# Another list order for one decoder step on one core: accumulator chains kept together, and eight small rows issued by ScalarE

## The chip, the cores and the metric

The kernel runs on one core of a Trainium2 chip. The metric is the device time of one execution in microseconds (us), as the median over runs. A core has five engines with instruction queues of their own: TensorE (PE in the profile; PEld is its weight load), VectorE (DVE), ScalarE (ACT), GpSimd (POOL) and SyncE (SP), which only issues transfers. SP, ACT and POOL can issue DMA transfers; the program chooses which.

## What is computed

One layer of a hybrid decoder, for a prompt of 512 tokens and for 8 sample rows of one token each, with model width 1024, all in f32:

```python
gate, q, k, v, z_att, logf, u, z_ssm = _pre(x, c, ...)   # adaLN RMSNorm, one projection, its columns split
o_att = fox_attention(q, k, v, logf)                     # 8 heads of 64, score bias from cumulated log-gates
y_ssm, h = s5_scan(u, h0, ...)                           # 32 groups, 64 complex states each
att = o_att * silu(z_att)
g   = gelu(y_ssm);  ssm = g * sigmoid(g @ w_glu + b_glu) * silu(z_ssm)
x   = x + gate * (concat(att, ssm) @ w_out)
y   = rmsnorm(x, g_final)
```

In prompt attention the score of query t and key s is `q·k/8 + cum[t] − cum[s]`, where `cum` is the running sum of the log-gates. Each sample row attends to 4096 cached positions, found through a page table, and to itself. The outputs are y, k, v, log-gates and the last states, for the prompt and for the sample.

## The kernel before, in words

**An order by list scheduling.** The body, `tile_fox_s5_step`, is written as plain generators: `prompt()` (norm, projections of q, k, v, u and the gates, S5, attention, output projection) and `decode()` (the sample rows). Their instructions are not issued at once. `Engine` records each call in a `Plan`, with the regions it reads and writes, a modelled duration and the ring buffers it uses. `Plan.order()` then picks the order: a simulation with a ready heap for each engine, where an engine that comes free takes the ready operation with the smallest key. The key is the operation's place in the written program, less `BEHIND` times the work that depends on it, plus `TURN[i // GRP]`, one number for each group of 20 operations. For PE there is one exception: if the smallest key asks for another tile shape (rows by columns of the array, each 32, 64 or 128) than the last product, PE takes a product of the present shape instead, provided its key is at most `STAY` greater. `LAT` holds for each engine two latencies: to a successor on another engine, and on the same one. A transfer is put off if 8 of its queue are under way. `Plan.issue()` emits everything in that order on line 381 (385 in the changed kernel), so every instruction of the profile carries this line, and groups are told apart by their tiles. The order within an engine is fixed in the program; engines meet only through semaphores, and an engine executes in order.

**The parts named later.** PSUM tiles are `mm` (two buffers, projections and outputs), `tr` (two, transposes), `s2` (one, scores, shown as `s`), `sm` and `pv` (one each). `hT` is the normalised transposed prompt, `w` and `qk` are weight buffers (the latter also hold q and k), `cs` the transposed conditioning vectors. `arA` and `arB` are two large SBUF areas, of which pieces are lent out by turns.

**Decode.** For each of 64 chunks of 1 MB (8 rows × 8), POOL gathers K rows by an indirect transfer (`kidx` holds the row numbers). DVE multiplies the chunk by the broadcast q (`kv<-kv,qs`, 128x2048) and reduces it to scores (`sc<-kv`). After the softmax, POOL gathers V chunks, and PE accumulates them in `pv`, four products of 128 rows by 32 columns each, in four column quarters. The broadcast q is itself a product, `sm<-qsp,s4b`, copied to `qs` by ACT. Gathers of the cached log-gates (`suf<-in_cache_logf_dram,lidx`) and their suffix sums give the score bias. Chunks lie in three `kva` buffers, and later also in pieces of arA.

**Prompt attention** (`attn`, from line 1174). DVE makes `cum` by a scan (line 1185) over transposed log-gates. For each pair of heads, m = 0 to 3, ACT copies q and k of two heads into two 66-row tiles in arB (line 1197), and a transfer (line 1198) puts two rows of `cum`, 4 KB, into row 64 of the q tile and row 65 of the k tile (eight transfers in all, `arB<-arA 1x2x512`, issued from SP). The products for the scores (`s2<-arB`) read these 66 rows. ACT takes exponentials, PE transposes them, and PE multiplies by v into an `mm` tile.

**The start.** The adaLN modulation is a product of `cs` with four slabs of `w_ada`, on `w_88` and `w_89` among them, in four column quarters. POOL raises the mean squares to the power −1/2 (`arA<-arA,nhalf`), ACT scales x by that, and PE transposes it (`tr<-ident,kv`).

Of the kernel before, what the change touches and what calls it, by code (L numbers as in the profile page):

```python
# [37 lines left out]
BEHIND = 0.0005  # L38
STAY = 150
GRP = 20  # L40
XAT = 5
TURN = [
# [6 lines left out]
]  # L49
# [22 lines left out]

LAT = {"PE": (200, 5), "DVE": (190, 127), "ACT": (165, 200), "Pool": (90, 100), "SP": (90, 0)}
ACT_SET = {AF.Exp: 0, AF.Silu: 1, AF.Sin: 1, AF.Gelu_apprx_tanh: 2, AF.Sigmoid: 3, AF.Identity: 1}
# [50 lines left out]
class Plan:  # L125
# [108 lines left out]
    def order(self):  # L234
# [24 lines left out]
        ready = {e: [] for e in engines}  # L259
        queue = deque(), deque()  # L260
        cols, loaded, hw = {}, 0.0, 0.0
# [24 lines left out]
        while done_n < n:  # L286
# [31 lines left out]
            if op.dma:  # L318

                q = queue[e == "Pool"]  # L320
                while q and q[0] <= t:
                    q.popleft()
                if len(q) >= 8:
                    heapq.heappush(waiting[e], (q[0], i))
                    continue
# [25 lines left out]
            if op.lock:  # L351
                t = max(t, port)
                port = t + c
            start[i] = t
            if op.func is not None and op.func != func:
# [4 lines left out]
            if op.dma:  # L360
                dma_free = max(dma_free, fin + 650) + op.dma
                fin = dma_free + 980
                queue[e == "Pool"].append(dma_free + 930)
            end = max(end, fin)
# [24 lines left out]
def tile_fox_s5_step(ctx, tc, x_prompt, x_sample, c_prompt, c_sample, cache_k, cache_v, cache_logf,  # L389
# [140 lines left out]
    t = trt()  # L530
# [643 lines left out]
    def attn(rp, ap):  # L1174
# [17 lines left out]
        for m in range(4):  # L1192
            qa, ka = qk
            for j in range(2):
                x = qk[j]
                for hh in range(2):
                    acopy(x[0:64, hh], res["qk"][j][64 * hh:64 * hh + 64, m])
                SP.dma_start(x[64 + j:65 + j], cum[2 * m:2 * m + 2])
            t = trt()
# [460 lines left out]
```

## Time and profile before

| what | value |
| --- | --- |
| time before, median of 3 runs | 613.65 us (605.77 to 616.77) |
| the profiled execution's own time | 612.74 us |
| span of its trace, first to last instruction | 610.7 us |
| mean granted PE clock | 0.933 |
| busy: PE, DVE, POOL, ACT | 529.8, 485.6, 227.6, 159.5 us |
| moved by DMA | 176.41 MB, mean 289 GB/s |

In the profile an instruction group reads "engine, operation, out<-in by the program's tile names without buffer numbers, shape, count". A bracket behind a timeline row is the engine's idle time just before it, and what ended it. The chain is followed back from the last instruction: each step goes to what released it. A 128x512 f32 product leaves two records. PE's granted clock is 1.00 at full speed.

### The profile page before, as it was taken

The numbers are of one execution on the slowest core, as the hardware profiler recorded it, in microseconds if no ns is written. First come the engines' busy times: TensorE is split into PE (matmuls) and PEld (weight loads), VectorE is DVE, ScalarE is ACT, GpSimd is POOL, SyncE is SP. The second block draws the span as 40 slices with busy tenths as digits, with TensorE's granted clock in tenths as the row PEclk, the third lists the DMA queues.
The fourth block names the chain that finished last, engine by engine and source line by source line (L and its number), as shares of the span: only waits on it lengthen the run. The fifth ranks groups of instructions, "written<-read, shape, count | busy, mean of one in ns | idle before, by whom it ended". The sixth has DMA issues, their size and how long they took to land.

```text
span 610.7 us, 7345 instructions
## 1 busy us (share of the span) xinstructions
PE 529.8 (87%) x2858; PEld 233.7 (38%) x2858; DVE 485.6 (80%) x687; ACT 159.5 (26%) x294; POOL 227.6 (37%) x172
## 2 busy tenths in 40 slices
PE   5538899999999798978887799889989989999993
PEld 2104477533333234646323344334334333333231
DVE  7985987997999999889562999886979376998514
ACT  4224303211001110150212563551542653000101
POOL 6670101452354133234411366324534251553400
PEclk9955989999999798999987899989968999999997
DMA  7996303583897659689695689988999999689940
GB/s 225 398 378 228 140 2 138 174 298 149 284 355 290 242 188 411 240 304 420 257 419 187 255 319 386 385 321 312 357 411 381 348 367 406 261 320 388 384 188 36
DMA packets 45195, 176.41 MB, mean 289 GB/s; under 512 B 6933, under 2 KB 21497, under 8 KB 27753
## 3 DMA queue, kind: packets, MB, share of 16 engines
q0 software_dynamic: 19264, 135.74, 57.6%
q1 hardware_dynamic: 25392, 39.44, 18.3%
q10 hardware_dynamic: 504, 0.78, 0.4%
q8 instruction: 22, 0.36, 0.2%
q14 instruction: 13, 0.10, 0.0%
HBM read 171.48 MB, written 4.42 MB: 288 GB/s over the span
## 4 chain that ended last, share of the span: by engine, by line
PE 41%; DVE 26%; DMA 16%; ACT 6%; issue 5%; POOL 3%; SPq 2%; DVEq 0%; POOLq 0%; ACTq 0%
PE mm L381 27%; DVE arA L381 9%; DVE sc L381 8%; PE pv L381 6%; DVE kv L381 5%; DMA kv<-in_cache_v_dram,kidx 5%; PE tr L381 4%; DMA arB<-arA 3%; DMA kv<-in_x_prompt_dram 3%; DMA out_dram<-e 2%; POOL arA L381 2%; ACT L381 2%; DMA arA<-in_cache_v_dram,kidx 2%; SPq L381 2%; PE s L381 2%
## 5 line engine op out<-in xcount | busy, mean ns | idle before, releaser
L381 PE MATMUL mm<-hT,w 128*128 128x512 f32 x256 | 134.6, 630 | 0.1
L381 DVE TENSOR_TENSOR kv<-kv,qs 128x2048 f32<-128x2048 f32 x38 | 86.4, 2280 | 15.0 <-DMA kv<-in_cache_k_dram,kidx 12.4
L381 POOL DMA_INDIRECT kv<-in_cache_v_dram,kidx x38 | 56.0, 1474 | 94.4 <-PE pv L381 36.3
L381 DVE TENSOR_REDUCE sc<-kv 128x32 f32<-128x2048 f32 x38 | 86.0, 2273 | 0.2
L381 POOL DMA_INDIRECT kv<-in_cache_k_dram,kidx x38 | 48.0, 1262 | 82.6 <-PE pv L381 36.7
L381 POOL DMA_INDIRECT arA<-in_cache_v_dram,kidx x26 | 50.5, 1941 | 67.2 <-DVE sc L381 55.5
L381 POOL DMA_INDIRECT arA<-in_cache_k_dram,kidx x26 | 39.0, 1498 | 95.5 <-PE pv L381 52.7
L381 DVE TENSOR_TENSOR arA<-arA,qs 128x2048 f32<-128x2048 f32 x26 | 59.2, 2279 | 2.9 <-DMA arA<-in_cache_k_dram,kidx 1.8
L381 DVE TENSOR_REDUCE sc<-arA 128x32 f32<-128x2048 f32 x26 | 59.1, 2275 | 0.2
L381 PEld LDWEIGHTS mm<-hT,w 128*128 128x128 f32 x256 | 41.9, 195 | 27.5 <-issue 22.8
L381 ACT ACT_TABLE_LOAD x31 | 39.8, 1283 | 36.5 <-DMA q_s<-in_x_sample_dram 11.1
L381 PE MATMUL pv<-kv,arA 128*32 128x512 f32 x304 | 42.1, 613 | 5.8 <-DMA kv<-in_cache_v_dram,kidx 5.8
L381 PE MATMUL s<-arB 128*32 128x128 f32 (+4 forms) x240 | 35.2, 306 | 7.0 <-DMA arB<-arA 5.6
L381 DVE TENSOR_TENSOR arA<-arA 128x512 f32<-128x512 f32 (+8 forms) x105 | 37.2, 378 | 0.6
L381 PE MATMUL mm<-w,hT 128*128 128x256 f32 x128 | 37.3, 410 | 0.0
L381 PE MATMUL pv<-arA 128*32 128x512 f32 x208 | 31.1, 655 | 6.6 <-DMA arA<-in_cache_v_dram,kidx 3.6
L381 ACT ACTIVATE arB<-tr 128x512 f32<-128x512 f32 (+3 forms) x44 | 20.3, 477 | 54.8 <-PE s L381 27.5
L381 PE MATMUL mm<-w,arB 128*128 128x512 f32 x64 | 33.2, 610 | 0.0
L381 PEld LDWEIGHTS s<-arB 128*32 128x32 f32 (+1 forms) x240 | 23.3, 152 | 24.5 <-issue 14.1
L381 PE MATMUL mm<-qk,arB 128*128 128x512 f32 x64 | 32.3, 607 | 0.0
L381 PE MATMUL mm<-qk,hT 128*64 128x256 f32 x256 | 32.1, 404 | 0.0
L381 PE MATMUL tr<-ident,arB 128*128 128x128 f32 (+1 forms) x102 | 24.4, 302 | 8.5 <-ACT arB L381 8.5
(244 smaller groups left out, 717.5 us busy)
## 6 DMA issues: line engine op xcount, KB each, us to landing
w<-in_w_in_dram SPq DMA_DIRECT2D x10, 1024.0 KB
w<-in_w_ada_dram SPq DMA_DIRECT2D x9, 1024.0 KB
qk<-in_w_ada_dram SPq DMA_DIRECT2D x2, 1024.0 KB
kv<-in_x_prompt_dram SPq DMA_DIRECT2D x2, 1024.0 KB
qk<-in_w_in_dram SPq DMA_DIRECT2D x2, 1024.0 KB
qk<-in_w_out_dram SPq DMA_DIRECT2D x2, 1024.0 KB
w<-in_w_out_dram SPq DMA_DIRECT2D x2, 1024.0 KB
hT<-in_x_prompt_dram SPq DMA_DIRECT2D x1, 2048.0 KB
```

The costliest lines, as they stand in the source:

```text
L381: fn(*args, **kw)
```

## The change

Five edits, none of which adds, removes or alters an operation, its operands or its arithmetic:

- `STAY` is 80 in place of 150, and all 113 numbers of `TURN` are others, on the whole larger in size.
- PE's latency to its own successor is 0 in place of 5. In the heap of `order()`, the next product of a chain is then ready at the moment PE chooses, and its key is close to that of the product before.
- The model of the DMA queues has one queue for each engine, where SP and ACT shared one.
- A transfer that POOL issues is modelled as held while DVE has the port that both use.
- The rows of `cum` are issued from ACT (`A`) and not from SP.

```diff
-STAY = 150
+STAY = 80
 GRP = 20
 XAT = 5
 TURN = [
-    -872, -5579, -1925, -3047, -2630, -3562, -2038, -2939, -2200, -1386, -1903, -48, -3522, -654, -1143, -30,
+    -7694, 3784, 245, 1458, -775, -289, 127, -5585, 3014, -1233, -3, -966, 1188, -487, -8884, 491, 5234, 987,
...
-LAT = {"PE": (200, 5), "DVE": (190, 127), "ACT": (165, 200), "Pool": (90, 100), "SP": (90, 0)}
+LAT = {"PE": (200, 0), "DVE": (190, 127), "ACT": (165, 200), "Pool": (90, 100), "SP": (90, 0)}
...
-        queue = deque(), deque()
+        queue = {e: deque() for e in engines}
...
-                q = queue[e == "Pool"]
+                q = queue[e]
...
             if op.lock:
                 t = max(t, port)
                 port = t + c
+            elif op.dma and e == "Pool":
+
+                c += max(0.0, port - t)
...
-                queue[e == "Pool"].append(dma_free + 930)
+                queue[e].append(dma_free + 930)
...
-                SP.dma_start(x[64 + j:65 + j], cum[2 * m:2 * m + 2])
+                A.dma_start(x[64 + j:65 + j], cum[2 * m:2 * m + 2])
```

What it does to the built programs is seen in the order of instructions on each engine. Three places follow; a number behind a name is the tile's number, and xN stands for N like instructions in a row.

PE, in the third head pair of prompt attention, before. `mm_413` is a gate projection, `s2_415` scores, `tr_408` and `tr_409` transposes (all of 128 by 128 tiles), `pv_359` V chunks (128 by 32):

```order
L381 MATMUL mm_413<-hT_110,w_380 128x512
L381 MATMUL pv_359<-kv_358,arA_78 32x512 x4
L381 MATMUL tr_408<-ident_91,arB_79 128x128
L381 MATMUL mm_413<-hT_110,w_380 128x512
L381 MATMUL pv_359<-arA_78 32x512 x4
L381 MATMUL tr_409<-ident_91,arB_79 128x128
L381 MATMUL mm_413<-hT_110,w_380 128x512
L381 MATMUL s2_415<-arB_79 128x128
L381 MATMUL mm_413<-hT_110,w_380 128x512
L381 LDWEIGHTS identb_95
L381 MATMUL s2_415<-maskb_96,identb_95 128x128
```

And the same place now:

```order
L385 MATMUL mm_413<-hT_110,w_380 128x512
L385 MATMUL tr_408<-ident_91,arB_79 128x128
L385 MATMUL mm_413<-hT_110,w_380 128x512
L385 MATMUL tr_409<-ident_91,arB_79 128x128
L385 MATMUL mm_413<-hT_110,w_380 128x512 x6
L385 MATMUL s2_415<-arB_79 128x128
L385 LDWEIGHTS identb_95
L385 MATMUL s2_415<-maskb_96,identb_95 128x128
L385 MATMUL s2_415<-arB_79 128x128 x2
```

The chain of `mm_413` and that of `s2_415` no longer alternate, and the two groups of V products between them have gone to a later place, where two such groups stand together.

PE, at the broadcast of the first sample row's q (`sm_150<-qsp_124,s4b_123`), before. `mm_166` to `mm_169` are the projection of u:

```order
L381 MATMUL mm_168<-qk_117,hT_110 64x256
L381 MATMUL mm_168<-qk_118,hT_110 64x256
L381 LDWEIGHTS s4b_123
L381 MATMUL sm_150<-qsp_124,s4b_123 128x512
L381 MATMUL mm_168<-qk_117,hT_110 64x256
```

And now:

```order
L385 MATMUL mm_166<-qk_117,hT_110 64x256
L385 MATMUL mm_166<-qk_118,hT_110 64x256
L385 MATMUL mm_156<-e2_155,s4_98 8x512
L385 LDWEIGHTS s4b_123
L385 MATMUL sm_150<-qsp_124,s4b_123 128x512
L385 MATMUL mm_166<-qk_117,hT_110 64x256
```

The broadcast stands behind the first two products of `mm_166`, where before it stood behind all of `mm_166` and `mm_167` and most of `mm_168`; in rows of PE it has gone from the 201st to the 76th.

SP, around the first two rows of `cum`, before:

```order
L381 DMA w_300<-in_w_in_dram 128x8x256
L381 DMA out_3_dram<-arA_78 128x4x512
L381 DMA w_301<-in_w_in_dram 128x8x256
L381 DMA arB_79<-arA_78 1x2x512 x2
L381 DMA out_8_dram<-arA_78 8x512
```

And ACT now, where they stand between activations of the S5 part:

```order
L385 ACTIVATE e2_276<-mm_275 128x256
L385 ACTIVATE arA_78<-mm_277 8x256
L385 ACT_TABLE_LOAD
L385 ACTIVATE arB_79<-mm_279,gcol_103 128x512
L385 DMA arB_79<-arA_78 1x2x512 x2
L385 ACTIVATE arB_79<-mm_282,gcol_103 128x512
L385 ACTIVATE arB_79<-mm_286,gcol_103 128x512
```

The other six rows of `cum` stand on ACT each behind the copies of q or k into the same tile (`arB_79<-qk`).

POOL does both of its powers ahead of the gathers `suf`, where all eight gathers came before the second power, and DVE computes `kidx` and `lidx` behind the first modulation of the sample rows, where it did so among its first instructions. At the start of PE's stream both `mm_111<-w_88,cs_102` and `mm_111<-w_89,cs_102` stand behind transposes of x (`tr_127<-ident_91,kv_85`), where `w_88` stood ahead of them.

11 rows, old and new, of the table TURN are left out of this document.

## The prediction

> **What bounds the kernel now.** I read the shares of the page first, then busy time by stage, then the chain of waits, and last the timelines of the places the change touches.
>
> ```profile
> PE 529.8 (87%) x2858; PEld 233.7 (38%) x2858; DVE 485.6 (80%) x687; ACT 159.5 (26%) x294; POOL 227.6 (37%) x172
> PE 41%; DVE 26%; DMA 16%; ACT 6%; issue 5%; POOL 3%; SPq 2%; DVEq 0%; POOLq 0%; ACTq 0%
> ```
>
> TensorE (PE) is busy for 87% of the span and carries most of the chain that ended last; VectorE (DVE) comes next with 80%, and transfers hold 16% of the chain. An average hides which of them rules where, so here are five stages (columns: us of the stage, then busy us and instructions of PE, weight loads, DVE, ACT and POOL, the granted PE clock, the share of the DMA engines and GB/s):
>
> ```profile
> 0.00:75.00 75.00, 46.31 (x370) 21.25 (x370) 61.94 (x198) 24.69 (x39) 33.53 (x37) 0.80 0.80 279
> 75.00:300.00 225.00, 207.83 (x1297) 104.73 (x1298) 204.59 (x287) 39.18 (x68) 79.63 (x50) 0.97 0.66 245
> 300.00:330.00 30.00, 21.87 (x69) 7.99 (x67) 12.04 (x9) 3.72 (x6) 3.75 (x4) 0.84 0.81 321
> 330.00:596.00 266.00, 249.28 (x1106) 98.61 (x1101) 201.04 (x185) 89.45 (x176) 109.18 (x77) 0.96 0.88 339
> 596.00:610.70 14.70, 4.47 (x25) 1.11 (x24) 6.01 (x11) 2.47 (x5) 1.48 (x4) 0.75 0.10 38
> ```
>
> Up to 75 us DVE leads (61.9 of 75). From 75 to 300 PE and DVE are both nearly full: PE idles 225 − 207.8 = 17.2 us, DVE 20.4. From 300 to 330 nothing is full, which is a stall. From 330 to 596 PE alone is full (249.3 of 266, 16.7 us idle), with DVE at 201. So time can come out of the PE's stream after 330 us, out of the stall, and, between 75 and 300 us, only to the extent that PE and DVE both have less to do or less to wait for.
>
> **No work is taken away.** Both programs have the same products, DVE instructions and table loads; the change only orders them otherwise and sends eight small rows through another queue. Four things follow.
>
> **1. Fewer changes of tile shape on PE.** Counted in the built orders, the accumulator changes from one product to the next 960 times before and 392 times now; the tile shape (rows by columns of the array: 128 by 128, 128 by 32 for the V products, and so on) changes 452 times before and 240 now. These two must be priced apart, and one piece of the PE's timeline does it:
>
> ```profile
> 553.33 1.02 PE L381 MATMUL mm<-qk,arB 128*128 128x512 f32 x2
> 554.19 1.02 PE L381 MATMUL mm<-w,arB 128*128 128x512 f32 x2
> 555.14 1.07 PE L381 MATMUL pv<-kv,arA 128*32 128x512 f32 x8
> 556.14 1.12 PE L381 MATMUL mm<-w,arB 128*128 128x512 f32 x2
> 557.10 1.02 PE L381 MATMUL mm<-qk,arB 128*128 128x512 f32 x2
> 557.96 1.02 PE L381 MATMUL mm<-w,arB 128*128 128x512 f32 x2
> 559.68 1.02 PE L381 MATMUL mm<-w,arB 128*128 128x512 f32 x2
> ```
>
> The rows with qk and with w go into two different accumulators, with the same tile shape. From 553.33 to 554.19 is 0.86 us, and from 557.10 to 557.96 again 0.86: alternating accumulators costs nothing (the f32 product leaves two records each time). So the change's most visible effect, chains that stay together, is worth 0.00 where the shape stays. A visit to the V products in between costs something: 554.19 to 555.14 is 0.95 instead of 0.86, so 0.09 for one change; and from 554.19 to 557.96 is 3.77 us for three products (3 × 0.86) and one V group (some 0.87, since four column quarters run side by side), 0.32 more than 3.45, so 0.16 for each of the two. I take 0.12 for a change, with 0.10 and 0.16 as ends.
>
> Where the changes go matters more than their number. 136 of the 212 stand before the stall and 71 behind it. Behind it PE is full: 71 × 0.12 = 8.5 us, of which I count 8, since part of the 16.7 us of idling there (waits on ACT and gathers) stays where it is; ends 71 × 0.10 = 7.1 and 71 × 0.16 = 11.4. Before it, 136 × 0.12 = 16 us of PE leaves a stretch in which DVE is as full as PE, so it comes out in point 3.
>
> **2. The stall at 318 to 330 us.** Prompt attention starts with products that need the rows of cumulated log-gates in partitions 64 and 65 of arB. Timeline and chain, in order of time:
>
> ```profile
> 296.01 0.39 SPq L381 DMA_DIRECT2D w<-in_w_in_dram  x1
> 296.52 1.21 DVE L381 TENSOR_TENSOR_SCAN arA<-ones,tr 8x512 f32<-8x512 f32 x1 [1.34 <-PE tr L381]
> 297.75 8.95 SPq L381 DMA_DIRECT2D arB<-arA  x2
> 304.11 19.71 DMA arB<-arA
> 308.40 2.29 DVE L381 TENSOR_TENSOR kv<-kv,qs 128x2048 f32<-128x2048 f32 x1 [5.55 <-DMA kv<-in_cache_k_dram,kidx]
> 323.95 0.77 PE L381 MATMUL s<-arB 66*128 66x128 f32 x2 [5.56 <-DMA arB<-arA]
> ```
>
> The scan that makes the rows ends at 297.7. SP, which has just issued a weight load of 1 MB, needs 8.95 us to issue two rows of 4 KB, and the rows land about 323.9, 26 us behind the scan. PE idles 5.56 us for them. It then pays again:
>
> ```profile
> 316.70:323.60 6.90, 1.70 (x10) 0.30 (x2) 4.54 (x3) 0.60 (x1) 0.00 (x0) 1.00 0.91 357
> 323.60:330.40 6.80, 6.45 (x18) 2.71 (x19) 1.29 (x4) 0.69 (x1) 0.00 (x0) 0.50 0.14 17
> 330.40:337.20 6.80, 6.80 (x30) 3.43 (x26) 2.08 (x6) 3.87 (x10) 1.88 (x2) 1.00 0.98 354
> ```
>
> After the window with 1.70 us of work the clock is 0.50 for 6.8 us, so that what was done there would have taken half: 3.4 us. The stall costs 5.56 + 3.4 = 9 us.
>
> The change issues the rows from ACT. What does ACT's queue need? Nothing of this kind goes through it before, and there are two sets of rows to bound it, the other six cum rows on SP and a pair of small loads on ACT:
>
> ```profile
> L381 SPq DMA_DIRECT2D arB<-arA x8: 564/958/6301, 297.8 to 443.9; - x8
> 258.77 0.80 ACTq L381 DMA_DIRECT2D arB<-in_b_ada_dram  x2
> 262.31 0.63 ACT L381 ACTIVATE arB<-qk 64x512 f32<-64x512 f32 x1 [4.55 <-DMA arB<-in_b_ada_dram]
> ACT L381 <- DMA q_s<-in_x_sample_dram: 11.1, 1, 11.1
> ```
>
> Issues take 0.56 to 6.3 us on SP, with a median of 0.96; a pair on ACT took 0.80, and its data were used 3.5 us after the issue (258.77 to 262.31). The other small ACT load was waited for 11.1 us. So the rows should be there 1 + 3.5 to 1 + 11 us behind the scan: 4.5 to 12. In the new order some 14 us of PE's stream (by the same prices) lies between the transposes that feed the scan and the first product that needs the rows; before it was about 20, since PE ran dry at 318.4. The cover is thinner, the rows quicker: the wait goes, and with it the cold clock. What is late next is DVE, which waited 5.55 us for a K chunk at 308.40 and had 12 us of work in 30. I take 8 of the 9 us, with 0 and 9 as ends.
>
> A page bears on this from the other side. The Trainium skill, "Trainium Kernel Development and Optimization", section "Key Constraints", says that transfers issued from SP, ACT and POOL all run on the same 16 DMA engines, and that issuing from several only saves issue time. The window with a DMA share of 0.91 fits it, and by it only the 9 us of issue would go; whether the rest of the lateness stays is a rival below.
>
> ACT is in order, and takes on eight issues. The first pair stands between two activations of the S5 part, the others each behind the copy that writes the same tile, which already waits for that tile's last reader; so they add no wait for a buffer, only their issue, six or so of 0.6 to 1 us on an engine with 89 of 266 us busy. No charge.
>
> **3. The decode begins earlier.** The first multiply of a K chunk needs the broadcast q, a product out of qsp:
>
> ```profile
> 75.87 0.42 DVE L381 CAST qsp<-e 8x512 bf16<-8x512 f32 x1
> 77.42 14.49 PE L381 MATMUL mm<-qk,hT 128*64 128x256 f32 x116
> 98.61 0.39 PE L381 MATMUL sm<-qsp,s4b 72*128 72x512 bf16 x1
> 99.67 2.29 DVE L381 TENSOR_TENSOR kv<-kv,qs 128x2048 f32<-128x2048 f32 x1 [0.47 <-ACT qs L381]
> ```
>
> qsp is there at 76.3, and PE makes the product at 98.6, behind a long projection. Now it stands ahead of that projection, so that the first K chunk can be multiplied from about 80, some 20 us earlier, and DVE work that stood ahead is put behind. DVE has 20.4 us of idling in 75 to 300, and PE 17.2 plus 16 from point 1; since the two must both shrink, the gain is 0 at least (the idle places move) and 16 at most. DVE's sum stays 204.6 and K chunks still wait for gathers, so I am near the lower end: 6.
>
> **4. The start.** One step goes the other way. The modulation needs the sums over both halves of w_ada before the first normalised rows are made.
>
> ```profile
> 33.67 10.22 POOL L381 TENSOR_SCALAR arA<-arA 128x4 f32<-128x4 f32 x1 [6.49 <-ACT hT L381]
> 37.08 1.94 PE L381 MATMUL mm<-w,cs 128*32 128x512 f32 x8 [1.09 <-DMA w<-in_w_ada_dram]
> 43.97 1.04 POOL L381 TENSOR_TENSOR arA<-arA,nhalf 128x4 f32<-128x4 f32 x1
> 48.73 1.93 PE L381 MATMUL mm<-w,cs 128*32 128x512 f32 x8
> 52.54 0.37 DVE L381 TENSOR_TENSOR arA<-tr,arA 128x72 f32<-128x72 f32 x2 [8.72 <-PE tr L381]
> ```
>
> One such group of four products ran at 37.08 while PE had nothing else, the other at 48.73 on the path, behind transposes of x that wait for POOL's reciprocal root (10.22 us for 128 by 4 values, up to when DVE's row of two-input operations ends). In the new order both groups stand behind the first transposes: 1.93 us more on the path. At best the group finds a gap again: 0. At worst POOL's second step is held as the first was and the group waits behind a further copy, 1.04 + 1.04 us: 4. I take 2. The gathers move as well. POOL had done its suffix gathers, 1.26 us apart, early on:
>
> ```profile
> 21.03 0.95 POOL L381 DMA_INDIRECT suf<-in_cache_logf_dram,lidx  x1 [0.30 <-issue]
> 22.29 0.96 POOL L381 DMA_INDIRECT suf<-in_cache_logf_dram,lidx  x1 [0.30 <-issue]
> ```
>
> Now they follow the second root and the index arithmetic, which DVE does behind the first modulation, by its place in the order an estimated 62 to 70 us. Six of them, 1.26 us apart, the K gather and its landing come before the first multiply: another reason for "about 80", and for no more than 6 in point 3.
>
> **Sum.** 2 − 6 − 8 − 8 = −20 us, from a span of 610.7 to 590.7. The profiled execution took 612.74, 2.04 around its span, so 592.7; it lies 0.9 under the median of the runs (613.65), so the figure stands for a median too: 593. The ends give 0 − 16 − 9 − 11.4 = −36.4 (576) and 4 − 0 − 0 − 7.1 = −3.1 (610).
>
> **Rivals.** *The savings are swallowed.* DVE stays as full as it was before 300 us, and waits for gathers as it did at 308.40 (5.55 us); point 3 is worth nothing, of the stall only the cold clock goes (3.4), and behind it 8 less the start's 2: −9.4, so 603, or 606 if the cold clock stays as well. For it: DVE at 204.6 of 225 and DMA shares of 0.66 to 0.88. Against: behind 330 us PE is the only full engine. Chance 0.17.
>
> *The rows land no sooner.* If they wait for what is already under way on the DMA engines and not for SP, they land 26 us behind the scan as before, and PE has work for 14: a wait of 12 in place of 5.56. That is 6.4 lost and 8 not gained: 607. For it: the DMA share of 0.91 just ahead. Against: the three later pairs on SP, for none of which PE waited, and ACT's 3.5 us. [...] Chance 0.10.
>
> *The decode starves at first.* If index arithmetic and gathers on POOL are held by DVE as the root was for 10 us, the first K multiply comes about 10 us after 99.67 and not 20 before it: 6 not gained and 10 lost, 609. For: the 10.22 us above. Against: by then DVE has other work to fill that time. Chance 0.10.
>
> *ACT is stopped by its new transfers: slower.* If a pair takes 8.95 us to issue on ACT as it did on SP, the exponentials behind it wait, and PE needs those for its next transposes. Four pairs: 4 × 8.95 = 35.8, so 628. It decides from about 2 us a pair on, since ACT's slack covers less than that during a head pair. For: the 6.3 us of one row. Against: the median of 0.96 and 0.80 for the pair on ACT. Chance 0.08.
>
> That leaves 0.55 for the forecast, with its own range of 576 to 610.
>
> **Chances.** 2% is about what a measurement of this kernel can tell from no change: under 601.4 is faster, over 625.9 slower. The forecast falls under 601.4 in 0.50 of its 0.55, the rest is within 2%; the swallowed savings and the next two rivals, which end at 603 to 609, put 0.08 under, 0.24 within and 0.05 over, by what the rest of a table of new places may add; the last is slower, 0.08. Together 0.58, 0.29 and 0.13. For 8 in 10 the range goes from 576 to 616.
>
> **What would show it.** Point 1: V visits between products in fewer, longer groups, and PE busy over less than 249 us behind the first prompt scores, with the same count. Were alternating accumulators dear after all, PE would lose more than 12 us there. Point 2: no idle time of PE on arB's DMA, no window at 0.50 in mid kernel, and ACT issues under 1 us. Point 3: the first K multiply near 80. Point 4: the two adaLN groups both behind the copies of x, and DVE's idle gap longer than 8.72. I am wrong if PE's idle time between 75 and 596 grows, whoever it is that it waits for, or if the first K multiply is later than 99.67 and the end moves with it.

## The result, and the profile after

| | before | after |
| --- | --- | --- |
| median | 611.16 us (605.77 to 616.77, 4 runs) | 572.97 us (569.87 to 580.62, 4 runs) |
| ratio of the two, 95% interval | | 0.9386 (0.9267 to 0.9504) |
| profiled execution, its span | 612.74, 610.7 us | 571.23, 569.3 us |
| PE busy, idle | 529.8, 80.9 us | 490.2, 79.1 us |
| DVE busy, idle | 485.6, 125.1 us | 483.3, 86.0 us |

(Idle is the span less the busy time.) The change is faster by 6%, 38 us, where 20 was forecast; 573 lies 3 us under the range. Executions of one kernel lie up to 3.6% apart, so ratios, taken over the faster executions of each kernel, carry the verdicts below, and a span that was over 1.5% above the fastest execution of its kernel is marked *.

The page of the changed kernel, its busy times and its chain of waits:

```profile
PE 490.2 (86%) x2858; PEld 234.5 (41%) x2858; DVE 483.3 (85%) x687; ACT 158.4 (28%) x294; POOL 203.0 (36%) x172
PE 32%; DVE 32%; DMA 13%; issue 12%; POOL 5%; ACT 4%; DVEq 0%; POOLq 0%; ACTq 0%
```

PE's busy time is 39.6 us smaller with the same 2858 records, and its idle time hardly moved. DVE has the same work and 39 us less idle time. The chain was PE's before (41% to 26%); now it passes through PE and DVE alike.

By stages, cut at the first multiply of a K chunk and at the first prompt scores, before and after (columns as in the prediction's stages):

```profile
0.00:99.70 99.70, 69.55 (x545) 39.10 (x545) 79.47 (x257) 32.03 (x53) 34.47 (x38) 0.83 0.63 220
99.70:324.00 224.30, 200.47 (x1177) 92.26 (x1173) 198.19 (x235) 34.87 (x59) 82.45 (x53) 0.97 0.75 283
324.00:610.70 286.70, 259.75 (x1141) 102.33 (x1141) 207.94 (x196) 92.61 (x182) 110.66 (x81) 0.94 0.82 317
```

```profile
0.00:77.00 77.00, 50.23 (x457) 27.17 (x457) 66.66 (x193) 31.12 (x50) 30.67 (x38) 0.91 0.79 267
77.00:286.40 209.40, 183.89 (x1230) 97.82 (x1230) 199.52 (x296) 32.99 (x59) 68.40 (x50) 0.95 0.76 279
286.40:569.30 282.90, 256.05 (x1175) 109.46 (x1171) 217.10 (x200) 94.25 (x185) 103.92 (x84) 0.94 0.89 345
```

The first scores come 37.6 us earlier. The last stage is only 3.8 us shorter, but it holds more work than before (DVE 217 in place of 208 us, 34 more PE records), so its gain is not read off its length. DVE has the same work over the whole kernel, and its idle time falls in all three stages: from 20.2 to 10.3 us, from 26.1 to 9.9 and from 78.8 to 65.8.

The start, in the timeline after (in the prediction's rows POOL's TENSOR_SCALAR took 10.22 us, and DVE idled 8.72):

```profile
33.03 0.68 DVE L385 TENSOR_TENSOR arA<-arB,arA 128x512 f32<-128x512 f32 x1
33.58 0.20 POOL L385 TENSOR_SCALAR arA<-arA 128x4 f32<-128x4 f32 x1 [3.13 <-ACT hT L385]
33.63 1.89 DVE L385 TENSOR_TENSOR arA<-arA 128x512 f32<-128x512 f32 x3
33.86 1.33 POOL L385 TENSOR_TENSOR arA<-arA,nhalf 128x4 f32<-128x4 f32 x1
38.12 0.69 PE L385 MATMUL tr<-ident,kv 128*128 128x128 f32 x2
41.66 1.09 PE L385 MATMUL mm<-w,cs 128*32 128x512 f32 x8
52.58 1.13 POOL L385 DMA_INDIRECT suf<-in_cache_logf_dram,lidx  x1 [17.38 <-DVE lidx L385]
73.07 3.83 DVE L385 TENSOR_REDUCE arA<-suf 128x64 f32<-128x2048 f32 x1 [4.95 <-DMA suf<-in_cache_logf_dram,lidx]
77.03 2.27 DVE L385 TENSOR_TENSOR kv<-kv,qs 128x2048 f32<-128x2048 f32 x1
```

The same POOL operation takes 0.20 us, and the transposes of x start at 38.1. The first of them before:

```profile
46.25 0.48 PE L381 MATMUL tr<-ident,kv 128*128 128x128 f32 x1 [7.23 <-ACT kv L381]
```

The log-gate gathers wait 17.4 us for DVE's index arithmetic, as the prediction had it, though from 52.6 us on and not from 62 to 70; the first K chunk is multiplied at 77.0.

The 0.20 us are not a property of the new order. DVE's row of two-input operations runs beside it here too, from 30.6 to 44.5 us without a break. In two later runs that keep this order on DVE and POOL at the start (e7 and e9 below), the same instruction took 11.03 us, until that row had ended; in the profiles of the other seven runs with this start it took 0.20. In e7:

```profile
33.33 11.03 POOL L385 TENSOR_SCALAR arA<-arA 128x4 f32<-128x4 f32 x1 [3.13 <-ACT hT L385]
43.61 0.70 DVE L385 TENSOR_TENSOR arB<-arB,arA 128x512 f32<-128x512 f32 x1
46.70 0.47 PE L385 MATMUL tr<-ident,kv 128*128 128x128 f32 x1 [8.75 <-ACT kv L385]
53.70 0.37 DVE L385 TENSOR_TENSOR arA<-tr,arA 128x72 f32<-128x72 f32 x2 [9.39 <-PE tr L385]
85.78 2.27 DVE L385 TENSOR_TENSOR kv<-kv,qs 128x2048 f32<-128x2048 f32 x1
```

There the transposes start no sooner than before, DVE idles 9.39 us, and the first K chunk comes at 85.8. So 8 to 9 us of the early start in the profile above are not given by the order; they are luck, if frequent luck.

The rows of cum on ACT, and the first product that needs them:

```profile
272.75 1.20 DVE L385 TENSOR_TENSOR_SCAN arA<-ones,tr 8x512 f32<-8x512 f32 x1
273.99 1.31 ACTq L385 DMA_DIRECT2D arB<-arA  x2
286.42 0.49 PE L385 MATMUL s<-arB 66*128 66x128 f32 x2
```

All eight of them, by tile (durations in ns, least, median and most, then the first and the last start):

```profile
L385 ACTq DMA_DIRECT2D arB<-arA x8: 566/566/702, 274.0 to 396.3; - x8
```

A pair is issued in 1.31 us in place of 8.95, no row takes more than 0.70, and PE comes 12.5 us behind the scan without waiting.

### The profile page after: what moved, and what is told of

The parts are those of the page before. It is cut to its first block, busy times and chain, and to the rows that moved or that the text cites. A ratio compares the mean times of both kernels' runs of the same rounds, so it can differ in the third digit from the quotient of the medians.

```text
span 569.3 us, 7358 instructions
## 1 busy us (share of the span) xinstructions
PE 490.2 (86%) x2858; PEld 234.5 (41%) x2858; DVE 483.3 (85%) x687; ACT 158.4 (28%) x294; POOL 203.0 (36%) x172
## 4 chain that ended last, share of the span: by engine, by line
PE 32%; DVE 32%; DMA 13%; issue 12%; POOL 5%; ACT 4%; DVEq 0%; POOLq 0%; ACTq 0%
PE mm L385 20%; DVE arA L385 13%; DVE sc L385 8%; DMA kv<-in_cache_v_dram,kidx 6%; DVE kv L385 5%; PE pv L385 5%; DVE arB L385 3%; DMA arA<-in_cache_v_dram,kidx 3%; PE s L385 3%; DMA arA<-in_cache_k_dram,kidx 3%; PE tr L385 3%; POOL kv L385 3%; POOL arA L385 2%; ACT arB L385 2%; ACT L385 1%
## 5 line engine op out<-in xcount | busy, mean ns | idle before, releaser
L385 PE MATMUL mm<-hT,w 128*128 128x512 f32 x256 | 120.5, 611 | 0.8 <-DMA w<-in_w_in_dram 0.8
L385 POOL DMA_INDIRECT kv<-in_cache_v_dram,kidx x38 | 49.2, 1294 | 99.9 <-DVE sc L385 44.0
L385 PEld LDWEIGHTS mm<-hT,w 128*128 128x128 f32 x256 | 46.4, 193 | 57.8 <-issue 55.6
L385 POOL DMA_INDIRECT kv<-in_cache_k_dram,kidx x38 | 51.4, 1353 | 49.4 <-PE pv L385 15.7
L385 POOL DMA_INDIRECT arA<-in_cache_v_dram,kidx x26 | 39.2, 1508 | 79.4 <-DVE sc L385 66.1
L385 POOL DMA_INDIRECT arA<-in_cache_k_dram,kidx x26 | 31.6, 1214 | 75.9 <-PE pv L385 55.2
L385 PE MATMUL pv<-kv,arA 128*32 128x512 f32 x304 | 45.4, 625 | 6.2 <-DMA kv<-in_cache_v_dram,kidx 6.2
L385 PE MATMUL mm<-w,hT 128*128 128x256 f32 x128 | 31.5, 386 | 0.0
L385 ACT ACTIVATE arB<-tr 128x512 f32<-128x512 f32 (+3 forms) x44 | 20.2, 475 | 37.1 <-PE tr L385 28.9
L385 ACT ACTIVATE e<-mm 128x512 f32<-128x512 f32 (+3 forms) x25 | 13.1, 526 | 53.5 <-PE mm L385 48.6
L385 PEld LDWEIGHTS mm<-qk,hT 128*64 128x64 f32 x256 | 25.2, 197 | 6.5 <-issue 2.4
```

Source lines behind the costliest of these rows:

```text
L385: fn(*args, **kw)
```

## The experiments

For all kernels together, the profiled execution is divided up by PE: its work at full clock (busy time, less half of the part that fell into intervals at half clock), the clock cost (that half), and its idle time. The three make the span. Changes of tile shape and of accumulator are counted in the built order.

| kernel | shape | accumulator | PE work | clock | idle | span | ratio to before |
| --- | --- | --- | --- | --- | --- | --- | --- |
| before | 452 | 960 | 500.5 | 29.3 | 80.9 | 610.7 | 1 |
| after | 240 | 392 | 469.0 | 21.2 | 79.1 | 569.3 | 0.9386 (0.9267 to 0.9504) |
| e1 before, latency 0 | 197 | 343 | 458.7 | 49.9 | 144.5 | 653.1 | 1.085 (1.0767 to 1.0932) |
| e2 after, latency 5 | 430 | 900 | 494.6 | 36.0 | 91.9 | 622.5 | 1.0259 (1.0176 to 1.0342) |
| e3 before, STAY 6000 | 268 | 859 | 472.7 | 49.6 | 138.3 | 660.6 | 1.0881 (1.08 to 1.0962) |
| e4 before, rows on ACT | 452 | 960 | 499.4 | 17.9 | 77.9 | 595.2 | 0.9957 (0.9916 to 0.9999) |
| e5 before, grouped | 324 | 849 | 480.1 | 39.4 | 90.7 | 610.2 | 1.0113 (1.0063 to 1.0163) |
| e6 after, split | 312 | 454 | 478.0 | 16.3 | 68.6 | 562.9 | 0.9343 (0.9276 to 0.9411) |
| e7 after, rows on SP | 240 | 392 | 468.9 | 24.2 | 83.3 | 576.5* | 0.9315 (0.925 to 0.938) |
| e8 after, STAY 150 | 242 | 382 | 468.0 | 31.7 | 101.4 | 601.0 | 0.9922 (0.9862 to 0.9982) |
| e14 old start, then new | 248 | 428 | 470.4 | 21.9 | 76.1 | 568.3 | 0.9391 (0.9302 to 0.948) |
| e16 old to scores, then new | 383 | 760 | 488.9 | 31.8 | 79.2 | 599.9 | 0.9726 (0.96 to 0.9852) |
| e18 before, less PE work | 446 | 934 | 483.6 | 42.1 | 97.0 | 622.7 | 1.0205 (1.0097 to 1.0313) |

One execution stands for each kernel. PE's work comes out alike in like orders; the clock cost and the idle time do not: e4 has the order of before but for the queue of the rows, its clock cost is 11.4 us lower, and by the ratio it is 2.6 us faster. A difference of 10 us in one of these two columns alone tells little.

**What a change of shape costs, and whether it sets the time (e1, e2, e3).** One number each:

```diff
-LAT = {"PE": (200, 5), ...      # e1: the kernel before
+LAT = {"PE": (200, 0), ...
-LAT = {"PE": (200, 0), ...      # e2: the changed kernel
+LAT = {"PE": (200, 5), ...
-STAY = 150                      # e3: the kernel before
+STAY = 6000
```

> The kernel before with one number altered: PE's latency to its own successor is 0 in place of 5, so that the next product of a chain is ready when PE chooses. The table of places, STAY, the model of the queues and the cum rows on SP are those of before. Counted in the built order: 197 changes of tile shape (before 452, the change 240) and 343 changes of accumulator (before 960, the change 392). Shape theory: a change of shape costs PE about 0.15 us, a change of accumulator nothing, and PE's time sets the end. The trace's PE busy time, with what ran at half clock counted half, falls from 500.5 by 255 x 0.15 = 38 to about 462 us, and the time to about 575. Place theory: the gain comes from the new table, by which the decode begins 23 us earlier (first K multiply at 77.0 in place of 99.7); then the time stays at 600 or above, whatever PE's busy time does. Accumulator theory: 41.4 us for 568 changes is 0.073 each, so 617 x 0.073 = 45 us less, about 566.

> The changed kernel with that one number put back: PE's latency to its own successor is 5. Everything else of the change stays, the new table and the rows on ACT among it. Counted: 430 changes of tile shape and 900 of accumulator. Shape theory: 190 x 0.15 = 28 us more PE time, 497 us busy at full clock in place of 469, and a time of about 600. Place theory: the early decode stays, so the time stays near 575. Accumulator theory: 508 x 0.073 = 37 us more, about 610.

> The kernel before with STAY at 6000 in place of 150: PE looks much further for a product of the present tile shape, and the chains alternate as before. Counted: 268 changes of tile shape, 859 of accumulator, so the one falls by 184 and the other only by 101. Shape theory: PE busy at full clock falls by 184 x 0.15 = 28 to about 473 us; the time falls too, to about 585, less what is lost by products that are put off too long. Accumulator theory: 101 x 0.073 = 7 us less PE time, 493, and about 604.

PE's work came out as the shape theory had it: 458.7 for 462 forecast, 494.6 for 497, 472.7 for 473. In e3 the accumulator changes 859 times and the work is 3.7 us above the changed kernel's, which the 28 more shapes explain; 467 more changes of accumulator cost nothing. From before to e1 it is 41.8 us for 255 changes, 0.164 each; from before to after 31.5 for 212, 0.149.

The time did not follow: the medians were 659.4, 623.8 and 662.0 us. Of the forecasts only the place theory's "600 or above" for e1 holds, and it did not say why; e2 and e3 lie outside all of them. e1 has the least PE work of these, and is 8.5% slower than before. The page of e1:

```profile
PE 508.6 (78%) x2858; PEld 242.1 (37%) x2858; DVE 485.5 (74%) x687; ACT 151.3 (23%) x288; POOL 210.0 (32%) x172
```

Its three longest kinds of waits of PE (us in total, times, longest):

```profile
PE pv L381 <- DMA kv<-in_cache_v_dram,kidx: 31.0, 9, 7.9
PE pv L381 <- DMA arA<-in_cache_v_dram,kidx: 30.1, 5, 14.0
PE pv L381 <- DVE arA L381: 15.2, 3, 10.4
```

And its last stage, from the first scores on:

```profile
293.70:653.10 359.40, 261.88 (x1138) 107.74 (x1136) 218.31 (x199) 83.85 (x175) 104.18 (x85) 0.82 0.70 268
```

PE waits 61 us for V chunks, no engine is full behind the first scores (PE 262 of 359 us), and the clock is 0.82 there. The rule that saves shapes was used with a table of places made without it, and V products wait for their gathers. Neither edit of the change, the rule or the table, is faster alone: the latency without the table gives 1.085, the table and the other edits without the latency 1.026.

**How close the table fits its rule (e8).**

```diff
-STAY = 80
+STAY = 150
```

> The changed kernel with STAY put back to 150, everything else as in the change. Counted: 242 changes of tile shape and 382 of accumulator, as many as in the change, but the order differs from some point on. Shape theory alone: same PE busy time (469), same time within 1%. Theory of the fitted table (a low count helps only if the table was made for exactly this rule, because the places decide how long PE idles): PE busy 469 again, idle time up from 79 to 100 or more, time 590 or more.

The theory of the fitted table held: the same PE work (468.0), 22 us more idle time and 10 more clock cost, 602.6 us in the median. One number of the rule, with the counts all but unchanged, costs 5 of the 6%.

**PE work taken away or added without a new plan (e5, e6).** Both edit the finished order of PE and leave the other engines' orders alone:

```diff
-        for i in self.order():
+        for i in self.shuffle(self.order()):
...
+    # e5: up to DEEP = 4 operations ys of one shape between x and z of another go ahead of x
+    if ops[z].mode == ops[x].mode and all(ops[y].mode == ops[pe[n - 1]].mode != ops[x].mode for y in ys):
+        if all(self.over(seq, pos, x, y) for y in ys):
...
+    # e6: y of another shape goes between its neighbours w and x of one shape
+    if ops[w].mode == ops[x].mode != ops[y].mode == ops[pe[n + 2]].mode and self.over(seq, pos, x, y):
```

> The kernel before in its own order, with one thing done to PE's order afterwards: where up to 4 products of one tile shape stand between two of another, they are put ahead of both, if nothing they need comes later. Products move by a few places, the other engines' orders are untouched, the table, STAY and the latencies are those of before. Counted: 324 changes of tile shape in place of 452 (128 fewer), 849 changes of accumulator in place of 960. Shape theory: 128 x 0.155 = 20 us less PE busy time at full clock (480), and since nothing else moved, most of it in the time: 592 to 598. Place theory (shapes save PE time, but only the new table turns it into time): PE busy falls to 480, its idle time grows by as much, and the time stays at 606 to 612.

> The changed kernel in its own order, with the opposite done to PE's order: where two neighbours of one shape are followed by one of another, the third is put between the first two if nothing forbids it. Counted: 312 changes of tile shape in place of 240 (72 more), 454 of accumulator in place of 392; the other engines' orders are untouched. Shape theory: 72 x 0.155 = 11 us more PE busy time at full clock (480 in place of 469), and 6 to 11 us more time, 579 to 584. Place theory: PE busy grows by 11 and its idle time falls by as much, 573.

The place theory held in e6 and nearly in e5, where half of the work comes back as clock cost and the median, 613.8, lies above its 612. In e5 20.4 us of PE work are gone, the profile shows 10.1 us more clock cost and 9.8 more idle time, and the time is 1.1% longer. In e6 9 us of PE work are added and 5 of clock cost and 10 of idle time are gone; the time is that of the changed kernel.

**The queue of the rows (e4, e7).** The order of the plan is kept in both, and only the issuing engine is another:

```diff
+    AQ = Engine(plan, "SP", nc.scalar)      # e4: planned as SP, issued by ACT
-                SP.dma_start(x[64 + j:65 + j], cum[2 * m:2 * m + 2])
+                AQ.dma_start(x[64 + j:65 + j], cum[2 * m:2 * m + 2])
```

> The kernel before in its own order on PE, DVE, ACT and POOL, with the eight rows of cum issued by ACT, at the places of the whole order at which SP issued them. Queue theory (point 2 of the prediction): PE no longer waits 5.56 us for the rows nor runs 6.8 us at half clock behind that, each issue takes under 1 us, and the time falls by 5 to 9, to 602 to 606. Rival: the rows wait for the DMA engines and not for SP, land 20 us or more behind the scan as before, and the time stays at 611. Second rival: another wait comes in its place (DVE waited 5.55 us for a K chunk there), same time though the wait for arB is gone.

> The changed kernel in its own order on all engines, with the eight rows of cum issued by SP, at the places of the whole order at which ACT issues them. Queue theory, by the run with the rows on ACT in the order before, which won 0.4%: they land later by some 9 us, PE waits for part of that at the first scores, and the time grows by 2 to 9 us, 575 to 582. Rival: in the new order other work covers it, 573.

In e4 the mechanism of point 2 is there, line by line. Its timeline, and the windows that answer to the stall's:

```profile
294.57 1.21 DVE L381 TENSOR_TENSOR_SCAN arA<-ones,tr 8x512 f32<-8x512 f32 x1 [0.90 <-PE tr L381]
295.81 1.37 ACTq L381 DMA_DIRECT2D arB<-arA  x2
306.20 2.29 DVE L381 TENSOR_TENSOR kv<-kv,qs 128x2048 f32<-128x2048 f32 x1 [5.30 <-DMA kv<-in_cache_k_dram,kidx]
314.41 0.39 PE L381 MATMUL s<-arB 66*128 66x128 f32 x2
```

```profile
307.00:313.90 6.90, 6.90 (x22) 2.46 (x21) 6.13 (x5) 1.69 (x3) 0.94 (x1) 1.00 1.03 420
313.90:320.70 6.80, 6.80 (x26) 2.83 (x25) 5.33 (x6) 3.66 (x8) 1.41 (x2) 1.00 1.02 401
```

No wait for the rows, no half clock, and DVE's 5.3 us for a K chunk stay. The profiled span is 15.5 us shorter, but by the ratio it is 0.4%, 2.6 us (0 to 5); the medians, 605.25 and 611.53, are 6.3 us apart, so the size is known only roughly. In e7 the ratio is no worse than the changed kernel's, so on ACT or SP is the same there: in the new order SP issues the rows 18 us behind its last weight load and needs 1.38 us for a pair:

```profile
261.32 0.40 SPq L385 DMA_DIRECT2D w<-in_w_in_dram  x1
278.17 1.20 DVE L385 TENSOR_TENSOR_SCAN arA<-ones,tr 8x512 f32<-8x512 f32 x1
279.39 1.38 SPq L385 DMA_DIRECT2D arB<-arA  x2
```

**Which engine's work counts (e9 to e12 on the changed kernel, e17 and e18 on the one before).** The order is kept; single instructions are issued twice, shortened or left out, so that e10, e12, e17 and e18 compute less than the layer:

```diff
+    k += 1                                              # K reductions on DVE
+    if k % 8 == 4: fn(*args, **kw)                      # e9: 8 of 64 twice
+    if k % 6 == 3: args = (args[0], args[1][:, :, :, 0:8])   # e10, e17: 10 of 64 over 8 of 64 columns
...
+    if k in PICK: fn(*args, **{**kw, "stop": True})     # e11: 21 first products of chains twice
+    if k in PICK: continue                              # e12, e18: 19 products inside chains left out
```

> The changed kernel in its own order, where every eighth of the 64 reductions of a K chunk on DVE is issued twice (same result): 8 x 2.27 = 18.2 us more work on DVE, nothing else. New theory, from the runs so far (PE's busy time at full clock fell by 20 us in the grouped order of before, and by 42 in the one with latency 0, and the time did not fall): DVE is the engine that sets the time, with a constant 483 to 486 us of work, and the time is that plus its idle time, 122 us before and 83 to 86 now. Then 18.2 us more DVE work show almost whole: 587 to 592. PE theory (PE is the fullest engine and sets the time): PE idles 79 us anyway, DVE idles 86, the extra work goes into the latter: 573 to 578.

> The changed kernel in its own order, where every sixth reduction of a K chunk reads an eighth of its columns (10 of 64, so these scores are sums over 8 of 64 products; all else is computed). About 10 x 1.9 = 19 us less work on DVE. DVE theory: 12 to 19 us less time, 554 to 561. PE theory: no change, 570 to 575.

> The changed kernel in its own order, where the first product of 21 chains of 128x512 f32 is issued once more ahead of the chain (the chain then starts anew, same result): 21 x 0.86 = 18 us more work on PE, no change of shape, nothing else. PE theory: 18 us more, 587 to 592. DVE theory: most of it goes into PE's 79 us of idle time and into products that now run at full clock, 573 to 580.

> The changed kernel in its own order without 19 of the products inside chains of 128x512 f32 (each leaves out a slab of 128 of the 1024 or 512 terms of a projection): 19 x 0.86 = 16 us less work on PE. PE theory: 12 to 16 us less time, 557 to 561. DVE theory: 0 to 4 less, 569 to 573.

> The kernel before in its own order, where every sixth reduction of a K chunk reads an eighth of its columns (10 of 64; these scores are sums over 8 of 64 products): about 19 us less work on DVE. If DVE sets the time in the order before as well, 12 to 19 us less than the kernel before; if PE alone sets it there, as the forecast had it behind 330 us, less than 6.

> The kernel before in its own order without 19 products inside chains of 128x512 f32 (each leaves out a slab of 128 terms of a projection): 16 us less work on PE, most of it behind the first scores. If PE sets the time there, as the forecast had it, 10 to 16 us less than the kernel before; if PE's idle time takes it up, as with the grouped order, less than 5.

| kernel | work, by the profiles | ratio to before | against the order's own ratio |
| --- | --- | --- | --- |
| e9 after | DVE +17.8 us | 0.9582 (0.9461 to 0.9704) | +2.1%, 12 us |
| e10 after | DVE −19.9 | 0.9214 (0.9119 to 0.931) | −1.8%, −11 us |
| e11 after | PE +17.3 | 0.9507 (0.9404 to 0.961) | +1.3%, 7 us |
| e12 after | PE −16.7 | 0.9237 (0.915 to 0.9324) | −1.6%, −9 us |
| e17 before | DVE −20.0 | 0.9907 (0.98 to 1.0013) | −0.9%, −6 us |
| e18 before | PE −16.9 | 1.0205 (1.0097 to 1.0313) | +2.0%, 13 us |

In the new order neither theory is right alone: DVE's work shows by some 0.6 of its size and PE's by some 0.5. The two intervals leave 1.6 to 1.8% on their quotient, so e9 and e10 are just clear of it, e12 lies at its edge and e11 within. e17 fits neither of its forecasts for certain: 0.9% by the ratio, from 2% less to nothing, and 10 us by the medians (606.2 and 616.6). In the order before, 17 us less PE work give no less time: 2% more by the ratio, 5 us more by the medians (621.2 and 616.6), as with the 20 of e5. Behind the first scores e5's profile takes 284.8 us and e18's 295.0, where the kernel before took 286.7. What PE does instead, in e18 at one place, first in windows (the last row is the same place in the kernel before):

```profile
448.00:457.80 9.80, 4.46 (x26) 1.54 (x26) 8.32 (x7) 5.81 (x11) 1.45 (x2) 1.00 1.03 411
457.80:464.60 6.80, 6.29 (x16) 1.50 (x16) 2.23 (x3) 0.00 (x0) 1.56 (x2) 0.50 1.05 409
443.00:453.20 10.20, 8.46 (x27) 2.99 (x28) 8.58 (x7) 6.17 (x12) 3.09 (x2) 0.50 1.04 407
```

and the same stretch in PE's timeline, with the last two rows from the kernel before, the same two products:

```profile
458.31 2.05 PE L388 MATMUL mm<-hT,w 128*128 128x512 f32 x2 [3.93 <-DMA w<-in_w_in_dram]
460.28 1.93 PE L388 MATMUL pv<-kv,arA 128*32 128x512 f32 x8
452.44 1.50 PE L381 MATMUL mm<-hT,w 128*128 128x512 f32 x2
453.87 1.06 PE L381 MATMUL pv<-kv,arA 128*32 128x512 f32 x8
```

SP issues these weights at 438.5 us, and PE is ready for them 15.9 us later, with the DMA engines full (1.03). It waits 3.93 us, and what follows runs at half clock (a V group takes 1.93 us in place of 1.06). Before, SP issued them at 433.7, PE came 18.7 us later and did not wait; but it had run at half clock just ahead (443.0 to 453.2). So at this place the work saved is spent on the wait, and the half clock is not new but comes later. Over the whole execution 16.9 us of work are gone, and the profile shows 12.8 us more clock cost and 16.1 more idle time. The Trainium skill, "TensorE: Matmul & The Clock Gate", section "What's actually happening", has the clock fall to half behind an idle window of some 3.4 us. This place agrees: PE is idle from 454.4 to 458.3, and the clock is 0.50 from 457.8 on.

**Where the gain lies (e13 to e16).** Two whole orders joined: the one up to a point, then the other's order for all that is left, rows on ACT in all four.

```diff
-        for i in self.order():
+        head, tail = plans[HEAD], plans["AB"[HEAD == "A"]]
+        got = set(head[:n])            # n: at the first DVE operation of over 2 us, or the first product on the rows of cum
+        for i in head[:n] + [i for i in tail if i not in got]:
```

> Two whole orders joined: the changed kernel's order up to its first multiply of a K chunk, and from there the order of before for all operations that are left, the rows of cum on ACT. Stage theory (each stretch of the new order brings its own part, read from DVE, whose work is the same: at 100 us of DVE work the new order is 8 us ahead, at 250 us 13, at 300 us 32, at the end 36): 8 us from the start and 3 to 6 from the rows on ACT, 596 to 600. Whole-order theory (an order only pays as a whole, since each place counts on all the others): 605 or more.

> The reverse: the order of before up to its first multiply of a K chunk, and from there the changed kernel's order for what is left, the rows on ACT. Stage theory: only the 8 us of the start are missing, 578 to 584. Whole-order theory: 595 or more.

> The changed kernel's order up to the first product of prompt attention that needs the rows of cum, and from there the order of before for what is left, the rows on ACT. Stage theory: the new order's lead at that point is 13 to 23 us, so 587 to 597, and with the rows' part a little less. Whole-order theory: 605 or more.

> The order of before up to the first product of prompt attention that needs the rows of cum, and from there the changed kernel's order for what is left, the rows on ACT. Stage theory: the lead that the new order makes behind that point, 36 less 13 to 23, so 13 to 23 us: 587 to 597. Whole-order theory: 605 or more.

By the ratios e13 is 2.9% faster than before (0.9709, from 0.9547 to 0.9871), e14 6.1% (0.9391) and e16 2.7% (0.9726): 18, 37 and 17 us. e15's four runs lay too far apart for a ratio. The medians were 603.7, 576.6, 595.7 and 600.4 us, with 616.1 for the kernel before in the same runs (the changed kernel's ratio would make it 578): 12, 40, 20 and 16 us. So, as far as medians tell, the new order is worth some 20 us up to the scores and 16 behind them, together nearly the 38 of the whole, and the gain comes by stages. In the median e14 and e15 are with the stage theory (e14 a little under it), e13 and e16 fall between the two forecasts.

The first cut lies earlier than meant. The first DVE operation that the model holds for over 2 us is not a K multiply but the reduction of the log-gates, `arA<-suf`, just ahead of it. From the two traces:

```profile
97.10 2.31 DVE L419 TENSOR_TENSOR kv<-kv,qs 128x2048 f32<-128x2048 f32 x1
83.46 2.27 DVE L419 TENSOR_TENSOR kv<-kv,qs 128x2048 f32<-128x2048 f32 x1
```

So e13 (the first row) has the new start but the late first K multiply, and e14 (the second) has the old start and an early one. The start does not add: e13 gains 12 to 18 us with it alone, 2 to 3 of them from the rows if they count as in e4, and e14 loses nothing without it.

## Why the prediction was wrong, point by point

*Direction and size.* Faster was right, by nearly twice the size: 593 forecast, 573 measured.

*Point 1, the price of a change of shape.* Right in kind: accumulators cost 0.00 (e3), shapes do. The price was 0.15 (0.125 in e6 to 0.164 in e1) and not 0.12, near enough within its ends of 0.10 and 0.16. The Trainium skill, "TensorEngine Tiling (Array Packing)", section "Key Properties", says that a change of tiling mode drains the engine, and gives no time for it; the runs give 0.15 us.

*The step that failed* is the one behind that: "it comes out in point 3", with 6 for the 136 changes ahead of the stall, and 8 for the 71 behind it. In the two profiles PE's work is 31.5 us less, the whole price of the 212 changes, with PE's idle time the same (80.9 and 79.1) and 8.1 us less clock cost; the three make the 41.4 us between the spans. By e15 and e16 the two halves are worth 20 and 16 us, where the forecast had 12 (6 + 8 − 2) and 8. I had put the first near its lower end because DVE's work and its waits for gathers would stay; the new places took 39 us of DVE's idle time away (125.1 to 86.0), 16 of them between the first K multiply and the first scores.

*Its reason was wrong as well.* The 8 us rest on this, that behind 330 us "PE alone is full", so that less PE work is less time. That fails in e5 and e18: with the order kept, 20 and 17 us less PE work over the whole kernel gave 1.1 and 2.05% more time. A PE that is 94% busy still hands over to ACT, DVE and gathers, and who finishes early waits; that is my reading of e18's wait, seen at one place. That the forecast came out on the right side is in part luck: the gain needs the new table and the new rule together (e1, e2, e8), and the forecast priced only the counts and three places of the new order.

*The sign I had named for being wrong* came, though the kernel is faster: from 75 us to some 14 us ahead of the end PE idled 42.0 us before (up to 596) and 45.1 after (up to 556).

*Point 2, the stall.* The mechanism was right (e4: the wait and the half clock are gone, issues of 0.57 to 0.70 us, no loss on ACT, K gathers late next). The term was mis-sized: 8 forecast, 2.6 (0 to 5) measured in the old order by the ratio, 6.3 by the medians, and nothing in the new one (e7), where SP's weight load stands 18 us ahead. The rival, that the rows land no sooner, is not borne out in e4: PE reached the scores 18.6 us behind the scan without waiting, where it had waited until 26. The Trainium skill, "Trainium Kernel Development and Optimization", section "Key Constraints", by which only issue time is saved, goes with e4: as an estimate, the rows then land 26 less the 7.6 us of issue saved (8.95 less 1.37) behind the scan, 18.4, and e4's 18.6 without a wait allows it.

*Point 3, the early decode.* The first K multiply came at 77.0, forecast 80. What it is worth stays open. It is not enough: e8 has it at 75.6 and is 0.8% faster than before. e14 has it 6.5 us later than the changed kernel and is as fast. No run moves it alone; e13, which was meant to have it, has it at 97.1.

*Point 4, the start.* Both adaLN groups stand behind transposes as said. In the profiled execution 2 lost was wrong in sign: POOL's root took 0.20 us and not 10.22, everything behind it came 8 us earlier, and DVE's gap of 8.72 us is gone. In e7, where the same order's root took 11.03, the forecast holds: DVE's gap is 9.39, longer than 8.72 as foretold, and the modulation 1.2 us later than before (53.70 for 52.54). So the term was right where POOL is held, and luck undid it in the profile. Whether that shows in the time is open: the profiles of e7 and e9, with 11.03, have spans of 576.5 and 590.7 us, the longest of their kernels' runs, but e14's has 10.98 us there and a span of 568.3. What holds POOL is not shown, since DVE's row of two-input operations runs beside it both times.

*The rivals.* None came. The nearest is the one in which the savings are swallowed: the old order does swallow a saving on PE (e5, e18), and the new one lets about half of it through (e12).

What stays open: why e5 and e18 are slower and not merely equal (the clock accounts for 10 and 13 us in one profile of each, the first hand-off that is missed was not found), which waits the new table and rule remove together, and how much of the gain a table for latency 5, searched anew, would have had.

## What to carry to other kernels

A saving on the busiest engine is worth its price only if the waits around it move too: before it is entered in a sum, take the work away in the order as it stands and see whether the time falls. Divide the span into work at full clock, clock cost and idle time of the engine: two kernels with nearly the same count of switches (after and e8) differed by 5% through the last two. A table of places and the rule that reads it are one thing; a rule is not judged with a table that was made for another.

## What was not expected of the hardware

A PE with less to do did not finish sooner: with 16.9 us less work the time grew by 2%, and the profile shows 12.8 us more clock cost (half-clock time 82.3 and 113.7 us of the spans) and 16.1 more idle time. A transfer of 4 KB took up to 6.3 us to issue 1.7 us behind a weight load of 1 MB in the same queue, and 0.7 us when that load was 18 us back. And one POOL instruction on 128 by 4 values took 0.20 us in one execution and 11.03 in another, with the same order on POOL and DVE.
